# Keeping a bf16 copy of streamed weights in HBM for later tiles, and a shorter chain to the first matmul, in an eight-core decoder step

## The chip, the cores and the metric

The kernel runs on all 8 cores of one Trainium2 chip. The time of a run is that of the slowest core, in microseconds of the device. A program on all 8 cores has a slower state, in which one die (cores 0 to 3, or 4 to 7) is granted a lower TensorE clock; such runs are named slow, and only fast runs are compared here.

## The reference

The reference is one inference step of a two-layer decoder. Each core takes one prompt of 2048 tokens; the 32 decode sequences of 8 tokens are shared out as well, so that each core has a small group of 32 sample tokens. Cut to what matters:

```python
D_MODEL = 1024; SEQ = 2048; FFN_DIM = 2688; GLA_RANK = 16

def rmsnorm(x, g):
    y = x * rsqrt(mean(x * x, axis=-1) + EPS); return y * g
def swiglu_ffn(x, w_in, w_out):
    g, u = split(x @ w_in, 2); return (silu(g) * u) @ w_out
# layer 0
x += 0.5 * swiglu_ffn(rmsnorm(x), ...)            # fi0, fo0 in the kernel's names
x += gla_mixer(rmsnorm(x), ...)                    # v, qk, r, o; a gate of low rank 16
x += 0.5 * swiglu_ffn(rmsnorm(x), ...)            # fi1, fo1
k, v = shared_kv(x, ...)                           # kv
# layer 1
x += 0.5 * swiglu_ffn(rmsnorm(x), ...)            # fi2, fo2
x += dilated_window_attention(rmsnorm(x) @ wq, k, v) @ wo
x += 0.5 * swiglu_ffn(rmsnorm(x), ...)            # fi3, fo3
# in the GLA: log_a = log_sigmoid((h @ w_lowrank) @ w_g2 + b) / 16
```

All inputs and all outputs are fp32; the kernel multiplies in bf16.

## The kernel before

The prompt of a core is cut into four tiles of 512 tokens, t0 to t3, which run in pairs: t0 with t1, then t2 with t3. In each pair the even tile leads by up to 24 weight units. The sample tile of 32 tokens uses the units of t0. Every tile needs every weight, and SBUF does not hold them, so each tile streams all of them from HBM. A unit is 128 partitions by 2048 columns (2688 for the FFN's output weights). A load issued by GpSimd (POOL) casts it from fp32 to bf16 on the way, into one of two rings of 12288 columns, one for even tiles and one for odd ones. A slot of the ring comes free when its users (`users`: one tile, or t0 and the sample tile) are done.

The order of the instructions on each engine is fixed when the program is built, by a scheduler with a cost model. So an edit can change the order of everything after it.

The units and their loads (cuts are marked `# ...`):

```python
    for t in range(4):
        def add_unit(kind, i, src, n, users=0, t=t):
            u = Unit(src, n, users or (1 if t else 2), (t, kind, i))
            u.kind = kind
            units[(t, kind, i)] = u
            order[t % 2].append(u)
# ...
    first = {(0, "fi0", k): [("x", "b0", 2 * k + 1)] for k in range(4)}
    for k in range(4):
        first[(1, "fi0", k)] = [units[(0, "fi0", 12 + 2 * k)].key]

    def weights(slot):
        # ... take the next stretch of the ring, wait until the units in it are done with
            yield need(lambda over=over: all(o.left == 0 for _, _, o in over))
        # ...
            yield O(PL, (lambda e, u=u, dst=dst: e.dma_start(out=dst, in_=u.src)),
                    first.get(u.uid, []), writes=[u.key], cost=1.0, dma="w%d_%d" % (slot, k % NWS), nbytes=u.n * 512)
            u.ready = True
```

The start: x of a tile is loaded in four parts by SP, squared by ACT, summed by a chain of DVE adds, and the sum over partitions is one matmul with ones:

```python
    def load_x(T, prev):
        # ...
            yield O(SP, (lambda e, q=q, w=w, src=src, ms=ms: e.dma_start(
                out=T.x[:, ms[0]:ms[-1] + 1, :].rearrange("p m n -> p (m n)"), in_=src[:, q * w:(q + 1) * w])),
                [after.key] if T.t == 1 else [], writes=[xk(T, m) for m in ms], cost=0.1, dma="x%s_%d" % (T.b, q), nbytes=w * 512)
        for m in range(8):
            yield from square(T, m)      # ACT square; for 512 tokens a DVE add to the running sum

    def norm_stats(T):
        # ...
        ms = [T.sum] if n == 512 else range(8)
        yield mm(PS[b][:, 0:n], [(ones, T.h[:, m, :]) for m in ms], [hk(T, m) for m in ms] + ["ONE"], b, n)
```

The low-rank gate and the sample tile's GLA output:

```python
    def gla(T):
        # ... 8 matmuls of 16 output columns, then 4 with 16 rows of contraction
        yield from mmh(T, (PS[b][0:16, :],), lambda kt, z: WLR[:, kt, :], ["WLR"], (b,), n)
        # ...
                yield mm(PS[b], [(WG2[0:16, hd * 128:(hd + 1) * 128], glr)], [gk, "WG2"], b, n)
    # sample tile, for each s of 4 groups of 8 tokens:
                for hd in range(4):
                    for f in range(2):
                        e.matmul(po[:, hd * 2 + f, :], lhsT=vv[:, hd * 256 + f * 128:hd * 256 + (f + 1) * 128], rhs=am[:, hd, c8], start=True, stop=False)
                        ins = e.matmul(po[:, hd * 2 + f, :], lhsT=S0b[:, hd, f * 128:(f + 1) * 128], rhs=qT[:, hd, c8], start=False, stop=True)
```

The softmax here doesn't subtract the row's maximum and nothing guards it: scores larger than these inputs give would overflow.

## Time and profile before

| | before |
|---|---|
| time, median of 3 runs | 2364.44 us (2363.14 to 2366.65) |
| HBM read, written, per core | 662.88 MB, 15.40 MB |
| TensorE busy, core 0 | 2306.4 of 2359.6 us |

The profile was taken of a run in the slow state, so I read core 0, which is on the die that kept its clock. The view of the cores gives the span and the mean granted clock of each:

```profile
core 0: 2359.6 us, clock 0.993
...
die 1 (median of its cores): 2576.0 us, clock 0.897
```

The page of core 0 of the kernel before. Part 1 is busy time with its share of the span. The DMA row gives the busy share of the 16 DMA engines in 40 equal slices, in tenths. Part 3 gives the queues (q0 is the casting loads that POOL issues, q1 the plain transfers) with packets, MB and share, and the HBM traffic of the core. Part 6 gives loads with their size and median time from issue to landing.

```profile
PE 2306.4 (98%) x14660; PEld 1129.2 (48%) x14660; DVE 1219.9 (52%) x2180; ACT 1172.5 (50%) x2316; POOL 317.2 (13%) x599
...
DMA  9996898888988989988999988888899989598793
...
q0 software_dynamic: 84032, 326.10, 83.6%
q1 hardware_dynamic: 17120, 28.25, 4.0%
...
HBM read 662.88 MB, written 15.40 MB: 287 GB/s over the span
...
ring<-wfi POOLq DMA_DIRECT2D x336, 512.0 KB, 9.1
```

TensorE is busy 98% of the span, and the DMA engines are about as busy for most of it. Two limits lie close together.

The table of stretches of core 0. Its columns are the stretch, its length, the busy time (and number of instructions) of PE, of its weight loads, DVE, ACT and POOL, then the granted clock, the DMA share and GB/s moved, counted at the SBUF side:

```profile
0.00:118.00 118.00, 97.42 (x741) 48.04 (x742) 60.89 (x129) 68.32 (x167) 22.00 (x45) 1.00 1.00 177
20.00:120.00 100.00, 98.03 (x726) 48.09 (x726) 53.82 (x114) 61.80 (x147) 14.95 (x29) 1.00 1.04 179
1250.00:1420.00 170.00, 157.40 (x770) 75.02 (x767) 62.62 (x94) 56.99 (x94) 21.14 (x40) 0.96 0.89 159
```

From 20 to 120 us the DMA share is 1.04 (the view adds up the times of the packets, so a full stretch can come out a little above 1). There the pair has just begun, and the ring of each tile is being filled. In the same stretch, the view of the DMA queues says what was moved (MB at the SBUF side; a q0 byte in bf16 is two bytes at HBM):

```profile
q0 software_dynamic: 4377, 15.61, 95.7%
q1 hardware_dynamic: 576, 2.10, 7.6%
...
ring<-wfi POOLq DMA_DIRECT2D x25, 512.0 KB, 14.0
```

That is 15.61 MB of weights and 2.10 MB of x.

The view of the waits of TensorE on core 0: what it waited for, us in total, times, longest.

```profile
PE pst L615 <- DVE h L628: 12.7, 2, 10.5
PE pst L615 <- DMA ring<-wfo: 12.2, 3, 10.1
...
PE pst L615 <- DMA ring<-wfi: 5.7, 6, 2.4
```

Of the first line, 10.5 us are the start, from a first small matmul at 7.4 us to 18.2 us. The view puts this wait down to the chain of adds, which ended at 18.1 us, but the first weights landed at 18.1 us too. Of the second, 10.1 us are a single stall: the timeline of TensorE (start, us, instruction, and in brackets the idle time before it with what ended it) shows it at 1333 us.

```profile
1314.81 8.58 PE L615 MATMUL pst<-r,ring 128*128 128x512 bf16 x39
1333.48 16.04 PE L615 MATMUL pst<-r,ring 128*128 128x512 bf16 x63 [10.09 <-DMA ring<-wfo]
```

For accounts of where time goes I use one more number, worked out from the matmul starts in the trace. Matmuls of 512 columns that run back to back start 216 ns apart. The **excess** is the sum of what the gaps between starts have over that figure (in proportion for fewer columns, 2.2 ns and 2.4 columns a ns, and not under 25 ns). It counts waits and slow matmuls alike. All of the core's matmuls at these gaps make 2269.3 us.

### The profile page before, as it was taken

To read this page: it belongs to the slowest core of one execution; us is meant where nothing else is said; L and a number is where in the kernel's file an instruction comes from. 1 tells how busy PE (TensorE), PEld (TensorE's weight loads), DVE (VectorE), ACT (ScalarE), POOL (GpSimd) and SP (SyncE) were. 2 spreads that over 40 slices of the span, in tenths; PEclk is the share of its full clock that TensorE was granted. 3 is DMA by queue.
4 is the path that set the end of the run, shared out by engine and by line. 5 is a ranking of instruction groups with operands and counts; after the bars stand their busy time and mean duration, and the time that the engine had idled before them with its cause. 6 is when DMAs were issued, how large, how long until landed. Compare 5 with 4: busy or idle time off the path is not lost.

```text
span 2589.4 us, 42668 instructions; the slowest of 8 cores (2351.7 to 2589.4 us)
## 1 busy us (share of the span) xinstructions
PE 2542.9 (98%) x14660; PEld 1190.5 (46%) x14660; DVE 1223.3 (47%) x2180; ACT 1177.0 (45%) x2316; POOL 317.7 (12%) x599
## 2 busy tenths in 40 slices
PE   7999999999999999999999989999999999999999
PEld 3445444544444444455444435444544444444444
DVE  4424464445533446646543243454466335653742
ACT  5524544463443246455453124533555533753642
POOL 1111111101111111111111011011111111111110
PEclk8888888888888889999998878888999999999999
DMA  9986788778867788998897787667789989689794
GB/s 190 150 122 108 128 133 120 113 105 122 135 115 127 123 146 146 169 159 134 157 156 133 151 139 125 108 117 114 137 153 166 167 153 172 116 138 156 145 173 93
DMA packets 101362, 357.08 MB, mean 138 GB/s; under 512 B 12528, under 2 KB 17440, under 8 KB 101024
## 3 DMA queue, kind: packets, MB, share of 16 engines
q0 software_dynamic: 84032, 326.10, 77.7%
q1 hardware_dynamic: 17120, 28.25, 3.6%
q8 instruction: 122, 2.00, 0.3%
q14 instruction: 88, 0.72, 0.1%
HBM read 662.88 MB, written 15.40 MB: 262 GB/s over the span
## 4 chain that ended last, share of the span: by engine, by line
PE 96%; DMA 3%; issue 1%; ACT 0%; DVE 0%; SPq 0%; ACTq 0%; POOL 0%; POOLq 0%; DVEq 0%
PE pst L615 92%; DMA ring<-wfo 1%; DMA ring<-wfi 1%; PE pst L1410 1%; DMA ring<-ck 0%; PE pst L1349 0%; PE pst L987 0%; PE pst L970 0%; PE pst L988 0%; PE pst L1371 0%; DMA x<-xp 0%; PE pst L1433 0%; PE pst L1375 0%; PE pst L957 0%; PE pst L863 0%
## 5 line engine op out<-in xcount | busy, mean ns | idle before, releaser
L615 PE MATMUL pst<-h,ring 128*128 128x512 bf16 x6144 | 1531.1, 410 | 4.1 <-DVE h L631 3.3
L615 PEld LDWEIGHTS pst<-h,ring 128*128 128x128 bf16 x6144 | 623.5, 103 | 804.9 <-issue 471.8
L615 PE MATMUL pst<-r,ring 128*128 128x512 bf16 x3136 | 780.9, 409 | 6.4 <-DMA ring<-wfo 6.4
L620 ACT ACTIVATE pb<-pb 128x512 f32<-128x512 f32 x856 | 534.8, 629 | 64.7 <-DVE pb L823 4.4
L620 ACT ACTIVATE pb<-pst 128x512 f32<-128x512 f32 (+1 forms) x472 | 278.8, 595 | 567.6 <-PE pst L615 560.7
L628 DVE TENSOR_TENSOR pb<-pb,pst 128x512 f32<-128x512 f32 x368 | 252.2, 686 | 547.3 <-ACT pb L620 539.4
L615 PEld LDWEIGHTS pst<-r,ring 128*128 128x128 bf16 x3136 | 318.5, 103 | 415.6 <-issue 232.7
L511 POOL DMA_DIRECT2D ring<-wfi x336 | 178.0, 530 | 1224.4 <-PE pst L615 1150.7
L620 ACT ACTIVATE h<-x 128x512 bf16<-128x512 f32 x192 | 119.0, 627 | 391.3 <-DVE x L631 305.0
L628 DVE TENSOR_TENSOR r<-pb,pst 128x512 bf16<-128x512 f32 x336 | 230.6, 687 | 46.2 <-DVE pb L628 40.3
L631 DVE SCALAR_TENSOR_TENSOR x<-pst,x 128x512 f32<-128x512 f32 x128 | 88.3, 690 | 261.7 <-PE pst L615 261.4
L631 DVE SCALAR_TENSOR_TENSOR h<-x,CF,pb 128x512 bf16<-128x512 f32 x224 | 150.8, 746 | 13.4 <-ACT pb L620 12.6
L511 POOL DMA_DIRECT2D ring<-wfo x128 | 67.7, 529 | 605.5 <-PE pst L615 496.7
L628 DVE TENSOR_TENSOR pb<-pb,h 128x512 f32<-128x512 f32 x120 | 82.4, 689 | 43.7 <-ACT h L620 42.6
L615 PE MATMUL pst<-ring,h 128*128 128x256 bf16 x640 | 86.9, 302 | 0.0
L620 ACT ACTIVATE spb<-pst 128x32 f32<-128x32 f32 (+2 forms) x111 | 21.7, 198 | 125.0 <-PE pst L615 124.4
L615 PEld LDWEIGHTS pst<-ring,h 128*128 128x128 bf16 x640 | 67.4, 107 | 18.6 <-issue 5.1
L615 PEld LDWEIGHTS pst<-hsb,ring 128*128 128x128 bf16 x1536 | 53.9, 97 | 40.6 <-issue 35.4
L615 PE MATMUL pst<-hsb,ring 128*128 128x32 bf16 x1536 | 54.4, 178 | 14.1 <-DMA ring<-wfi 14.0
L511 POOL DMA_DIRECT2D ring<-wgl x64 | 33.9, 531 | 260.7 <-PE pst L615 238.9
L624 ACT COPY r<-pst 128x512 f32<-128x512 f32 (+3 forms) x104 | 51.0, 491 | 23.6 <-PE pst L1375 11.4
L628 DVE TENSOR_TENSOR x<-x,pst 128x512 f32<-128x512 f32 x64 | 43.9, 686 | 29.8 <-PE pst L615 29.7
(151 smaller groups left out, 1113.6 us busy)
## 6 DMA issues: line engine op xcount, KB each, us to landing
ring<-wfi POOLq DMA_DIRECT2D x336, 512.0 KB, 7.4
ring<-wfo POOLq DMA_DIRECT2D x128, 672.0 KB, 8.0
ring<-wgl POOLq DMA_DIRECT2D x64, 512.0 KB, 6.7
x<-xp SPq DMA_DIRECT2D x16, 512.0 KB, 9.6
y_p<-x SPq DMA_DIRECT2D x32, 256.0 KB, 7.8
ring<-wqd POOLq DMA_DIRECT2D x12, 512.0 KB, 9.7
ring<-wod POOLq DMA_DIRECT2D x16, 384.0 KB, 8.8
ring<-wkv POOLq DMA_DIRECT2D x8, 512.0 KB, 8.3
```

The lines of the kernel that those rows point to most:

```text
L511: yield O(PL, (lambda e, u=u, dst=dst: e.dma_start(out=dst, in_=u.src)), first.get(u.uid, []), writes=[u.key], cost=1.0, dma="w%d_%d" % (s ...
L615: ins = e.matmul(out, lhsT=l, rhs=r, start=(start and i == 0), stop=(stop and i == last), skip_group_check=skip)
L620: return O(ACT, lambda e: e.activation(out=out, in_=in_, func=func, scale=scale, bias=bias), reads, writes, c_act(n))
L624: return O(ACT, lambda e: e.copy(out=out, in_=in_), reads, writes, c_act(n))
L628: return O(DVE, lambda e: e.tensor_tensor(out=out, in0=a, in1=b, op=op), reads, writes, c_dve(n, rate))
L631: return O(DVE, lambda e: e.scalar_tensor_tensor(out=out, in0=a, scalar=s, in1=b, op0=op0, op1=op1), reads, writes, c_dve(n))
L1410: ins = e.matmul(PS[bs[hp]][0:nk, rr * 64 + jj * 32:rr * 64 + jj * 32 + 32], lhsT=KT[hp * 64:hp * 64 + 64, jj, sl_(r, nk, 16)], rhs=T.QT[h ...
```

## The change

The intent: the sum of the weight bytes that the four tiles read is large, and it is read as fp32. After the change tile 0 reads fp32 and, as each unit lands, writes it back to HBM in bf16 (`keep`, issued by SP). Tiles 1 to 3 load the bf16 copies. A unit of tile 0 now has a third user, its copy, so its ring slot is held until the copy is done.

Three smaller parts go with it. The first squares alternate between ACT and DVE and are summed by eight ones-matmuls in place of the chain of adds, and x of tile 0 is loaded by the SP and ACT queues by turns. The low-rank gate's eight matmuls go to four groups of 32 output columns, and the four that follow contract over 128 rows. The sample GLA's 64 alternating matmuls become 8 and 32 of one shape each.

The diff, cut to its core (cuts are marked `...`):

```diff
-            u = Unit(src, n, users or (1 if t else 2), (t, kind, i))
+            u = Unit(src, n, users or (1 if t else 3), (t, kind, i))
             u.kind = kind
+            u.copy = None
+            if not users:
+                if t == 0:
+                    u.copy = nc.dram_tensor("bf_%s_%d" % (kind, i), [128, n], BF16, kind="Internal").ap()
+                else:
+                    u.src = units[(0, kind, i)].copy
...
+    def keep(u, k):
+        yield O(SP, lambda e: e.dma_start(out=u.copy, in_=u.ap), [u.key], [("bf",) + u.uid[1:]], cost=0.1, dma="k%d" % (k % NWS), nbytes=u.n * BFB)
+        u.left -= 1
...
+            bf = u.uid[0] > 0
             yield O(PL, (lambda e, u=u, dst=dst: e.dma_start(out=dst, in_=u.src)),
-                    first.get(u.uid, []), writes=[u.key], cost=1.0, dma="w%d_%d" % (slot, k % NWS), nbytes=u.n * 512)
+                    first.get(u.uid, []) + [("bf",) + u.uid[1:]] * bf, writes=[u.key], cost=1.0, dma="w%d_%d" % (slot, k % NWS),
+                    nbytes=u.n * (BFB if bf else 512))
+            if u.copy is not None:
+                TH.spawn(keep(u, k), -31)
...
-            yield O(SP, (lambda e, q=q, w=w, src=src, ms=ms: e.dma_start(
+            yield O(ACT if T.t == 0 and q % 2 else SP, (lambda e, q=q, w=w, src=src, ms=ms: e.dma_start(
...
+        if T.t == 0:
+            T.sum = None
+            for m in range(8):
+                if m % 2:
+                    yield stt(T.h[:, m, :], T.x[:, m, :], 1.0 / 1024, T.x[:, m, :], ALU.mult, ALU.mult, T.n, [xk(T, m)], [hk(T, m)])
+                else:
+                    yield act(T.h[:, m, :], T.x[:, m, :], AF.Square, T.n, [xk(T, m)], [hk(T, m)], scale=1.0 / 32)
+                done.add(("sq", T.nm, 0, m))
+            return
...
-        ms = [T.sum] if n == 512 else range(8)
-        yield mm(PS[b][:, 0:n], [(ones, T.h[:, m, :]) for m in ms], [hk(T, m) for m in ms] + ["ONE"], b, n)
+        ms = [T.sum] if n == 512 and T.sum is not None else range(8)
+        for m in ms:
+            yield mm(PS[b][:, 0:n], [(ones, T.h[:, m, :])], [hk(T, m), "ONE"], b, n, start=(m == ms[0]), stop=(m == ms[-1]))
...
-        yield from mmh(T, (PS[b][0:16, :],), lambda kt, z: WLR[:, kt, :], ["WLR"], (b,), n)
+        hn = T.hn
+        for kt in range(8):
+            yield need(lambda: ("h", T.nm, hn, kt) in done)
+            p = slice(kt % 4 * 32, kt % 4 * 32 + 32)
+            yield O(PE, (lambda e: e.matmul(PS[b][p, :], lhsT=WLR[:, kt, :], rhs=T.h[:, kt, :], start=(kt < 4), stop=(kt >= 4))),
+                    [hk(T, kt), "WLR"], [("ps", b)], 0.06)
...
-                yield mm(PS[b], [(WG2[0:16, hd * 128:(hd + 1) * 128], glr)], [gk, "WG2"], b, n)
+                yield mm(PS[b], [(WG2[:, hd * 128:(hd + 1) * 128], glr)], [gk, "WG2"], b, n)
...
+                ins = e.matmul(PS[b][:, m * n:(m + 1) * n], lhsT=vv[:, m * 128:(m + 1) * 128], rhs=am[:, m // 2, :], start=True, stop=True)
...
-                        e.matmul(po[:, hd * 2 + f, :], lhsT=vv[:, hd * 256 + f * 128:hd * 256 + (f + 1) * 128], rhs=am[:, hd, c8], start=True, stop=False)
-                        ins = e.matmul(po[:, hd * 2 + f, :], lhsT=S0b[:, hd, f * 128:(f + 1) * 128], rhs=qT[:, hd, c8], start=False, stop=True)
+                        ins = e.matmul(po[:, hd * 2 + f, :], lhsT=S0b[:, hd, f * 128:(f + 1) * 128], rhs=qT[:, hd, c8], start=True, stop=True)
```

More of the change, by code (lines that the diff above doesn't have):

```diff
@@ L321, in build @@
     wfi = din("wfi", [4 * NF, 128, 2048]); wfo = din("wfo", [32, 128, 2688])
-    wgl = din("wgl", [16, 128, 2048]); wlr = din("wlr", [128, 128]); gg2 = din("gg2", [16, 512])
+    wgl = din("wgl", [16, 128, 2048]); wlr = din("wlr", [128, 256]); gg2 = din("gg2", [128, 512])
     wkv = din("wkv", [2, 128, 2048]); wqd = din("wqd", [3, 128, 2048]); wod = din("wod", [4, 128, 1536])
@@ L338, in build @@
     SM = A("SM", [128, 8], F32)
-    WLR = A("WLR", [128, 8, 16], BF16)
-    WG2 = A("WG2", [16, 512], BF16)
+    WLR = A("WLR", [128, 8, 32], BF16)
+    WG2 = A("WG2", [128, 512], BF16)
     U = A("U", [128, 4, 256], F32)
@@ L480, in build @@
     NWS = 8
+    BFB = 280
     first = {(0, "fi0", k): [("x", "b0", 2 * k + 1)] for k in range(4)}
@@ L805, in gla @@
         (b,) = yield from get_banks(1)
-        yield from mmh(T, (PS[b][0:16, :],), lambda kt, z: WLR[:, kt, :], ["WLR"], (b,), n)
+        hn = T.hn
[4 more added lines that the diff above has]
+                    [hk(T, kt), "WLR"], [("ps", b)], 0.06)
         (gi,) = yield from pool.get("glr", 1, 1)
-        glr, gk = pool.aps[gi][0:16, 0:256].bitcast(BF16), pool.key(gi)
-        yield copy(ACT, glr, PS[b][0:16, :], n, [("ps", b)], [gk])
+        glr, gk = pool.aps[gi][:, 0:256].bitcast(BF16), pool.key(gi)
+        yield copy(ACT, glr, PS[b], n, [("ps", b)], [gk])
         put(b)
@@ L1029, in gla_s @@
         (b,) = yield from get_banks(1)
-        yield from mmh(T, (PS[b][0:16, 0:n],), lambda kt, z: WLR[:, kt, :], ["WLR"], (b,), n)
+        yield from mmh(T, (PS[b][0:16, 0:n],), lambda kt, z: WLR[:, kt, 0:16], ["WLR"], (b,), n)
         glr = KB[0:16, 896:928]
@@ L1093, in gla_s, with fi @@
         gv = [rk(T, ("gv", hd)) for hd in range(4)]
+        (b,) = yield from get_banks(1)
+        def fi(e):
+            ins = None
+            for m in range(8):
+                ins = e.matmul(PS[b][:, m * n:(m + 1) * n], lhsT=vv[:, m * 128:(m + 1) * 128], rhs=am[:, m // 2, :], start=True, stop=True)
+            return ins
+        yield O(PE, fi, [gk] + gv, [("ps", b)], c_mm(8, n))
+        yield copy(ACT, oT.rearrange("p m n -> p (m n)"), PS[b][:, 0:8 * n], 8 * n, [("ps", b)], [rk(T, "go")])
+        put(b)
         for s in range(4):
@@ L1106, in fo @@
                     for f in range(2):
-                        e.matmul(po[:, hd * 2 + f, :], lhsT=vv[:, hd * 256 + f * 128:hd * 256 + (f + 1) * 128], rhs=am[:, hd, c8], start=True, stop=False)
-                        ins = e.matmul(po[:, hd * 2 + f, :], lhsT=S0b[:, hd, f * 128:(f + 1) * 128], rhs=qT[:, hd, c8], start=False, stop=True)
-                return ins
-            yield O(PE, fo, [gk, ub.key] + gv, [("ps", b)], 1.68)
-            yield copy(ACT, oT[:, :, c8], po, 64, [("ps", b)], [rk(T, "go")])
+                        ins = e.matmul(po[:, hd * 2 + f, :], lhsT=S0b[:, hd, f * 128:(f + 1) * 128], rhs=qT[:, hd, c8], start=True, stop=True)
+                return ins
+            yield O(PE, fo, [gk, ub.key], [("ps", b)], 0.3)
+            yield tt(oT[:, :, c8], oT[:, :, c8], po, ALU.add, 64, [("ps", b), rk(T, "go")], [rk(T, "go")])
             put(b)
@@ L1585, in prologue @@
         yield O(PL, lambda e: e.dma_start(out=CB[:, 128:], in_=cbd[:, :]), [], ["CB"], cost=1.0, dma="c1", nbytes=(B_END - 128) * 512)
-        yield O(PL, lambda e: e.dma_start(out=WG2[:], in_=gg2[:, :]), [], ["WG2"], cost=1.0, dma="c2", nbytes=32768)
-        yield O(PL, lambda e: e.dma_start(out=WLR[:].rearrange("p a b -> p (a b)"), in_=wlr[:, :]), [], ["WLR"], cost=1.0, dma="c3", nbytes=65536)
+        yield O(PL, lambda e: e.dma_start(out=WG2[:], in_=gg2[:, :]), [], ["WG2"], cost=1.0, dma="c2", nbytes=262144)
+        yield O(PL, lambda e: e.dma_start(out=WLR[:].rearrange("p a b -> p (a b)"), in_=wlr[:, :]), [], ["WLR"], cost=1.0, dma="c3", nbytes=131072)
         yield O(SP, lambda e: e.dma_start(out=stabs[:], in_=rsd[:, :]), [], ["stabs"], cost=0.1, dma="c4", nbytes=32768)
@@ L1638, in make_in_maps @@
     shared = {
-        "wfi": f(wfi), "wfo": f(wfo), "wgl": f(wgl), "wlr": f(cols(glr, 8).reshape(128, 128)), "gg2": f(inp["gla_w_gate2"])[0],
+        "wfi": f(wfi), "wfo": f(wfo), "wgl": f(wgl), "wlr": f(np.pad(cols(glr, 8), ((0, 0), (0, 0), (0, 16))).reshape(128, 256)),
+        "gg2": f(np.tile(np.pad(f(inp["gla_w_gate2"])[0], ((0, 16), (0, 0))), (4, 1))),
         "wkv": f(np.stack([cols(kvw[:, i * 256:(i + 1) * 256], 8).reshape(128, 2048) for i in range(2)])),
```

## The prediction

> **What bounds the kernel now.** I read core 0, on the fast die of a slow run (2359.6 us, clock 0.993, view of the cores). TensorE is busy in 2306 of those us (table of stretches). 512-column matmuls start 216 ns apart; costing every matmul by its columns, I estimate 2286 us of bare TensorE work. About 60 us remain, beside 7 before the first matmul and 6 after the last:
> - start: tile 0's first FFN matmul runs at 22 us;
> - a 10.1 us wait for a wfo load (waits of TensorE) up to 1333 us, at a DMA share of 1.03; with the slow restart 16 us;
> - the sample GLA's 64 eight-column matmuls, 108 ns each, 7 us;
> - smaller DMA waits at 500 to 1000 us, 10 us.
>
> DMA is the second limit: in 22 to 115 us its share is 1.04, at 175 to 188 GB/s written, twice that read. The Trainium skill, "HBM Reference", Specifications, gives a core 358 GB/s; the trace agrees, at 360. A 512 KB unit (1 MB of fp32) then takes 2.9 us; TensorE uses one in 3.9 us, with the sample's matmuls.
>
> **What the change does.**
> 1. Tiles 1 to 3 read 2 bytes an element instead of 4; tile 0 writes 2 more. While tiles 0 and 1 run together HBM bytes are unchanged (4+2+2 against 4+4); in packets, 4 KB cast ones take 324 ns (median), plain ones 172: 668 against 648. In the second half the load halves.
>  - Removed: the stall at 1323 us, both tiles there now bf16: -15 us. Small DMA waits: -5.
>  - Added: at first tile 0 runs nearly alone. A unit costs 1.5 MB of HBM traffic, estimated 4.4 us against TensorE's 3.9. For 15 to 20 units TensorE becomes DMA-bound, until tile 1's cheap loads mix in: +6 us (0 to +15).
> 2. Start. TensorE sums the squares, in place of a DVE chain that ended at 18.1 us. But the first weights still wait for x, and the first two units land at 18.2 and 21.6 us, as the normalised x is ready (21.7). So only part counts: -3.
> 3. Low-rank gate: 8 matmuls of 16 output columns, 219 ns apart, become two sets of four in separate column groups. "TensorE: Matmul & The Clock Gate", Part 3, says that such tiles run concurrently; no run here shows it. From 7.9 us in all to some 2.5: -5. The 16-row gate matmuls (317 ns apart, 16) become 128-row ones (216): -1.5.
> 4. Sample GLA: 64 alternating 32- and 128-row matmuls become 8 and 32 of one shape: -5.
>
> **Sum.** -15 -5 +6 -3 -6.5 -5 = -28.5. Predicted **2336 us** (-1.2%), range **2312 to 2360**. Chances: faster by over 2% 0.13, within 2% 0.83, slower 0.04.
>
> **What would show it.** HBM reads fall from 663 to about 427 MB, writes rise from 15 to 94. DMA share in the second half about 0.5, no DMA wait of TensorE over 1 us there, none near 1320 us. Waits for wfi in 20 to 110 us grow from 0.3 us to several. First FFN matmul at 18 to 20 us. Gate matmuls on WLR about 60 ns apart.
>
> **What would make it wrong.** The added term is the least certain: copies may hold ring slots longer or slow the loads through the whole first half (+20), or the static order mixes tile 1 in early enough for no cost (-6). Column groups may not overlap (+5).

## The result, and the profile after

Ratios here and below are the mean time of one kernel's fast runs over that of the other's in the same rounds, so they are not quite the ratios of the medians that are quoted.

| | before | after |
|---|---|---|
| time, median | 2363.79 us (4 runs) | 2383.05 us (4 runs, one of them slow; the ratio also uses a fifth, fast run of 2379.07 us) |
| ratio of the fast runs | 1 | 1.0071, 95% interval 1.0052 to 1.0090 |
| HBM read, written | 662.88, 15.40 MB | 427.24, 94.04 MB |
| first matmul of 512 columns on FFN weights | 22.1 us (core 0; 20.0 to 22.1 over the cores) | 21.7 us (core 0; 19.8 to 22.2 over the cores) |

The change is slower, by 0.7%, where 1.2% faster had been predicted. The interval lies clear of 1, and the time lies outside the predicted range.

The profile after is of a fast run, and I read core 7, the slowest:

```profile
core 7: 2376.0 us, clock 0.985
die 0 (median of its cores): 2364.5 us, clock 0.989
```

The page of core 7 after the change, with the lines that answer to those above:

```profile
PE 2312.0 (97%) x14643; PEld 1130.3 (48%) x14643; DVE 1216.5 (51%) x2181; ACT 1166.6 (49%) x2309; POOL 317.1 (13%) x599
...
DMA  9999699988898989997755544444554563354452
...
HBM read 427.24 MB, written 94.04 MB: 219 GB/s over the span
...
ring<-wfi POOLq DMA_DIRECT2D x84, 512.0 KB, 14.0
...
ring<-bf_fo_3 POOLq DMA_DIRECT2D x12, 672.0 KB, 4.8
```

The traffic is just what was predicted: reads 427 MB, writes 94 MB. The DMA row falls to 4 to 6 tenths in the second half. Note the line of `ring<-wfi`: the fp32 loads, now only tile 0's, take 14.0 us to land where they took 9.1.

The stretches of core 7:

```profile
0.00:118.00 118.00, 81.05 (x574) 37.37 (x575) 46.73 (x102) 50.51 (x130) 16.19 (x34) 0.90 0.95 215
20.00:120.00 100.00, 78.03 (x567) 36.49 (x568) 43.73 (x93) 45.63 (x115) 9.51 (x18) 0.88 1.01 227
1250.00:1420.00 170.00, 170.00 (x834) 80.52 (x832) 69.36 (x103) 63.57 (x106) 22.69 (x44) 1.00 0.53 174
```

The stretch near 1320 us is now full (170.00 of 170.00 us, before 157.40), at a DMA share of 0.53. But in the first 118 us TensorE is busy 81.05 us where it was 97.42, and the granted clock there is 0.90 where it was 1.00. The DMA share is about 1 in both.

The DMA queues of core 7 from 20 to 120 us:

```profile
q0 software_dynamic: 3290, 11.03, 67.1%
q1 hardware_dynamic: 3307, 11.55, 33.3%
...
ring<-wfi POOLq DMA_DIRECT2D x15, 512.0 KB, 15.0
x<-xp SPq DMA_DIRECT2D x4, 512.0 KB, 21.1
```

Two of the loads on q0 are bf16 units (1.05 MB). So HBM carried 2 × 9.98 + 1.05 for the loads, and 11.55 for x (2.10) and copies (9.4): 32.6 MB, against 33.3 before. **The memory carried as much as before, but 9.4 MB of it were copies, and the weights that landed fell from 15.6 to 11.0 MB.** The Trainium skill, "HBM Reference", Specifications, gives a core about 358 GB/s; this trace is near it, at 326 to 333 GB/s, reads and writes added.

The waits of TensorE on core 7:

```profile
PE pst L632 <- DMA ring<-wfi: 16.8, 8, 6.4
...
PE pst L632 <- DVE h L645: 8.7, 1, 8.7
PE pst L632 <- DMA ring<-wfo: 3.9, 3, 3.3
```

The waits for `wfi` grew from 5.7 to 16.8 us (from 20 to 120 us alone, from 2.7 to 12.9), and the 10.1 us wait for `wfo` is gone. The wait of 8.7 us for h ends at 96 us, so it is new in the early stretch as well: it is the sum of squares of tile 1, whose x took 21.1 us to land (last line of the view of the queues above). A piece of the timeline of TensorE shows what such a wait can cost; its last two lines are from later on the same core:

```profile
36.33 0.55 PE L632 MATMUL pst<-hsb,ring 128*128 128x32 bf16 x16 [2.56 <-DMA ring<-wfi]
36.73 5.30 PE L632 MATMUL pst<-h,ring 128*128 128x512 bf16 x16
...
55.70 0.59 PE L632 MATMUL pst<-hsb,ring 128*128 128x32 bf16 x16 [6.36 <-DMA ring<-wfi]
56.12 6.00 PE L632 MATMUL pst<-h,ring 128*128 128x512 bf16 x16
...
62.37 3.61 PE L632 MATMUL pst<-h,ring 128*128 128x512 bf16 x16
...
618.42 0.55 PE L632 MATMUL pst<-hsb,ring 128*128 128x32 bf16 x16 [2.56 <-DMA ring<-wfi]
618.82 3.61 PE L632 MATMUL pst<-h,ring 128*128 128x512 bf16 x16
```

Sixteen matmuls of 512 columns take 3.61 us (the line at 62.37). After the wait of 2.56 us the same sixteen take 5.30 us, and after that of 6.36 us 6.00 us: of the first ten, most start 427 ns apart and not 216. The Trainium skill, "TensorE: Matmul & The Clock Gate", Part 1, describes this: after idling, the array runs at half rate for some microseconds. The trace agrees, but not after every wait: after another one of 2.56 us, at 618 us, the sixteen take 3.61 us. On core 7, from 20 to 120 us, six gaps of over 0.8 us between 512-column matmuls make 22.8 us of excess, and 43 matmuls at half rate another 8.8 us; before it was 11 such matmuls, 2.2 us, and no such gap.

The account of the whole, in us: the time to the first matmul, then the excess. Core 0 is taken for both, so that the same core is compared; in brackets the range over the six cores after the change whose trace has all matmuls.

| stretch, us | before, core 0 | after, core 0 (range) | difference |
|---|---|---|---|
| to the first matmul | 7.4 | 12.8 (11.0 to 12.8) | +5.4 |
| to 120 | 16.5 | 40.9 (32.5 to 40.9) | +24.4 |
| 120 to 290 | 12.0 | 1.2 (1.2 to 3.7) | -10.8 |
| 290 to 420 | 1.4 | 6.3 (5.5 to 10.8) | +4.9 |
| 420 to 1250 | 17.8 | 24.8 (15.9 to 24.8) | +7.0 |
| 1250 to 1420 | 18.3 | 0.8 (0.3 to 2.9) | -17.5 |
| 1420 to the end, with the tail after the last matmul | 17.2 | 18.1 (17.8 to 19.3) | +0.9 |
| matmuls at full rate | 2269.3 | 2270.2 | +0.9 |
| sum | 2359.9 | 2375.1 | +15.2 |

The sums agree with the spans, 2359.6 and 2374.7 us. So the gains came (near 1320 us, and from 120 to 290 us, where the sample GLA makes 5.6 of the 10.8 us), and the start, +29.8 us with its two rows, gave them all back. The question for the experiments is why the start costs 25 us or more where the prediction had 6.

### The profile page after: what moved, and what is told of

It reads as the page before. It is cut to its first block, busy times and chain, and to the rows that moved or that the text cites. A ratio compares the mean times of both kernels' runs of the same rounds, so it can differ in the third digit from the quotient of the medians.

```text
span 2376.0 us, 43134 instructions; the slowest of 8 cores (2353.5 to 2376.0 us)
## 1 busy us (share of the span) xinstructions
PE 2312.0 (97%) x14643; PEld 1130.3 (48%) x14643; DVE 1216.5 (51%) x2181; ACT 1166.6 (49%) x2309; POOL 317.1 (13%) x599
## 3 DMA queue, kind: packets, MB, share of 16 engines
q10 hardware_dynamic: 288, 1.05, 0.2%
HBM read 427.24 MB, written 94.04 MB: 219 GB/s over the span
## 4 chain that ended last, share of the span: by engine, by line
PE 91%; DMA 6%; DVE 1%; issue 1%; ACT 1%; POOL 0%; SPq 0%; DVEq 0%; ACTq 0%; POOLq 0%
PE pst L632 87%; DMA ring<-wfi 3%; DMA x<-xp 2%; DMA ring<-wfo 1%; PE pst L1453 1%; PE pst L1392 0%; DMA sts<-ring 0%; DMA ring<-wgl 0%; PE pst L1414 0%; PE pst L1004 0%; PE pst L1021 0%; DVE h L648 0%; PE pst L1022 0%; PE pst L1476 0%; ACT pb L637 0%
## 5 line engine op out<-in xcount | busy, mean ns | idle before, releaser
L632 PE MATMUL pst<-h,ring 128*128 128x512 bf16 x6144 | 1392.6, 382 | 3.2 <-DMA ring<-wgl 1.6
L632 PEld LDWEIGHTS pst<-h,ring 128*128 128x128 bf16 x6144 | 592.6, 98 | 710.0 <-issue 43.2
L632 PE MATMUL pst<-r,ring 128*128 128x512 bf16 x3136 | 711.5, 381 | 0.0
L632 PEld LDWEIGHTS pst<-r,ring 128*128 128x128 bf16 x3136 | 303.2, 98 | 358.7 <-issue 11.0
L525 POOL DMA_DIRECT2D ring<-wfi x84 | 44.5, 533 | 255.3 <-PE pst L632 155.9
L632 PE MATMUL pst<-ring,h 128*128 128x256 bf16 x640 | 75.4, 275 | 0.0
L632 PE MATMUL pst<-hsb,ring 128*128 128x32 bf16 x1536 | 53.3, 177 | 18.9 <-DMA ring<-wfi 16.8
L637 ACT ACTIVATE h<-pst 128x512 bf16<-128x512 f32 (+4 forms) x96 | 47.2, 514 | 19.3 <-PE pst L1392 11.0
L637 ACT ACTIVATE spb<-spb 128x32 f32<-128x32 f32 (+2 forms) x194 | 44.5, 230 | 14.7 <-ACT spb L637 0.8
```

The source lines that it names most:

```text
L632: ins = e.matmul(out, lhsT=l, rhs=r, start=(start and i == 0), stop=(stop and i == last), skip_group_check=skip)
L637: return O(ACT, lambda e: e.activation(out=out, in_=in_, func=func, scale=scale, bias=bias), reads, writes, c_act(n))
```

## The experiments

Three theories compete for the early loss:

- **Bytes.** Early on the memory has no spare time, so each byte of a copy pushes out a byte of a weight load.
- **Slots.** The copies hold ring slots longer, so loads are issued later; the number of bytes matters little.
- **Order.** The changed costs in the scheduler's model give another order of the program, and that order is worse.

Each kernel differs from the changed one only by the edits shown. All results were correct, all fast-run ratios are against the kernel before on the same chip, and all runs had five rounds. Line numbers in profile lines shift by some lines from kernel to kernel.

### No copies: e1_no_copy

Tile 0 writes nothing, all tiles load fp32; the start, the gate and the sample GLA stay changed.

```diff
-                if t == 0:
+                if False:
                     u.copy = nc.dram_tensor(...)
-                else:
+                elif False:
                     u.src = units[(0, kind, i)].copy
-            u = Unit(src, n, users or (1 if t else 3), (t, kind, i))
+            u = Unit(src, n, users or (1 if t else 2), (t, kind, i))
-            bf = u.uid[0] > 0
+            bf = False
```

> The change without its copies: all four tiles load fp32, and the shorter start, the gate matmuls and the sample GLA stay. Copy theories (bytes, or ring slots held): the idle time of TensorE in the first 118 us falls from 37 us back to about 20, the 10 us wait for a wfo load near 1320 us comes back, and the time is 2345 to 2358 us, below before. Start theory (x on two queues delays the first weights) or reorder theory (the new static order itself is worse): the time stays at 2370 us or above and the idle time in the first 118 us above 30 us.

Measured: ratio 0.9968 (0.9955 to 0.9981); its median, 2417 us, holds four slow runs of eight. TensorE is busy 94 to 101 us of the first 118, the excess to 120 us is 14 to 20 us, and the stall near 1320 us is back (13 to 15 us). So the early loss belongs to the copies and the cure of the late stall belongs to them as well. The rest of the change gains 0.3%.

### The first 18 units not copied: e3_skip18

```diff
+            skip = kind == "fi0" and i < 18
-            u = Unit(src, n, users or (1 if t else 3), (t, kind, i))
+            u = Unit(src, n, users or (1 if t else 2 if skip else 3), (t, kind, i))
-            if not users:
+            if not users and not skip:
```

(and `bf` is true only for a unit whose source is a copy)

> The change, but the first 18 FFN units, which tile 0 loads while it runs nearly alone, are not copied; tiles 1 to 3 read those 18 in fp32. Copy theories (bytes or slots): TensorE busy in the first 118 us rises from 81 to 95 us or more, no stall near 1320 us, and the time is 2330 to 2348 us (ratio to before 0.985 to 0.993). Start or reorder theory: within 6 us of the change as it is (about 2377 to 2383).

Measured: 2358.37 us, ratio 0.9977 (0.9965 to 0.9989). TensorE is busy 96 to 101 us of the first 118, as without copies. Near 1320 us the excess is 2 to 7 us. At 290 to 420 us it is 8 to 10 us, though, and the time is a miss: 2330 to 2348 us had been expected. The early loss is thus due to the copies of the very first units; but the other copies together gain nothing against no copies at all (0.9977 against 0.9968).

### x on one queue: e4_one_queue

```diff
-            yield O(ACT if T.t == 0 and q % 2 else SP, (lambda ...
+            yield O(SP, (lambda ...
```

> The change, but tile 0's x is loaded from the SP queue alone, as before. Start theory: the first weight unit is issued at about 10.5 instead of 12.2 us, lands near 18 us, and the time falls by 8 us or more. Bytes theory: the first FFN matmul comes 1 to 3 us earlier, but the stalls that follow take it back; the time changes by less than 4 us and TensorE busy in the first 118 us stays below 86 us.

Measured: 2375.49 us, ratio 1.0044 (1.0031 to 1.0057), against 1.0071 with two queues (on another chip), some 6 us less, between the marks that I had set for the two theories. It is not clear of noise: the two intervals overlap, and the other pairs that differ in the queues, also on different chips, give less or the reverse (without copies 0.9968 with two queues, e1, and 0.9958 and 0.9977 with one, e14 and e19; with 18 units uncopied 0.9977, e3, and 0.9987, e6). What the traces show is the start. The first matmul starts at 5.6 to 7.2 us where it started at 11.0 to 12.8, and the first one on FFN weights at 17.3 to 18.7 us where it was at 19.8 to 21.7. So the two queues delay the start by some 3 us; what they cost in all is not settled. The Trainium skill, "DMA: Bandwidth & Descriptors", section "Issuing engines are not separate DMA queues", says that transfers issued by several engines interleave on the same DMA engines and that only issue time is saved. The trace agrees: on two queues the two parts of x that ACT issued land first, at 8.80 and 11.57 us, and those of SP at 12.67 and 13.89 us (core 0 after the change), where before all four land in their order, at 9.89, 11.20, 12.47 and 13.63 us (core 0). So the last part comes no sooner, and the first one later, as it is one of SP's. The sample's x lands at 10.93 instead of 4.68 us, and the first weight load, which waits for the first part of x, is issued at 13.28 instead of 10.49 us.

### A write of the same bytes that holds no slot: e5, e9, e10

Here the first 18 units are not copied (as in e3), and each of them, when it has landed, sets off a write to HBM from tile 0's h buffer: as many bytes as the copy had (e5), half (e9), or an eighth (e10). No ring slot waits for it.

```diff
+    def fake(u, k):            # e5: 4 of h's 8 slices; e9: 2; e10: 256 columns of one
+        yield O(SP, lambda e: e.dma_start(out=scratch, in_=hb[0][:, 0:4, :]),
+                [landed(u)] + [h of tile 0], [], dma="k%d" % (k % NWS), nbytes=u.n * BFB)
```

> As the run that skips 18 copies, but each of those 18 units, once landed, sets off a write of as many bytes to HBM out of another tensor, so that it uses the DMA engines and HBM like a copy and holds no ring slot. Bytes theory: the early stall is back, TensorE busy in the first 118 us at 78 to 87 us and the time at least 12 us above the run without the writes. Slot theory (copies hold ring slots too long, bytes are harmless): busy at 93 us or more and the time within 5 us of the run without the writes.

> The same with every write cut to one half. Bytes theory with a threshold (a unit costs HBM time only where it exceeds TensorE's 3.9 us; half a copy makes it some 3.7 to 4.1): the time is closer to the run with small writes than to the one with full writes, at most 16 us above the former. Bytes theory without a threshold: half way between. Order theory: within 8 us of the full writes.

> The run with loose writes, with every one of the 18 writes cut to an eighth (512 bytes a partition for 4096); the order of every instruction on every engine is the same as in that run, only the size of these DMA differs. Bytes theory: the early stall is gone, TensorE busy in the first 118 us is 94 us or more, and the time is 2350 to 2366 us, at least 28 us under the run with full writes. Order theory (the static order of that run is itself worse): within 8 us of the run with full writes.

Measured: ratios 1.0134, 1.0082 and 1.0064 (intervals 1.0119 to 1.0149, 1.0069 to 1.0095 and 1.0048 to 1.0081). These runs failed as a test. DVE writes tile 0's next h into that same buffer, so it has to wait for the write to be done, and the trace shows it: TensorE waits 11.8 us for DVE's h in e10, and the chain of waits passes from the write to DVE. That wait is an artefact of the source that I chose, and it stays even with an eighth of the bytes. The falling ratio fits bytes, but does not show it.

### The same writes from a buffer that nobody overwrites soon: e11_writes_x and e12_tiny_x

The source is now x of tile 0, which is not rewritten in that stretch. e11 writes the bytes of a copy (4096 per partition), e12 an eighth (512). Both have the same instructions in the same order on every engine, and no slot is held in either. So they differ in bytes alone.

```diff
-        src = hb[0][:, 0:4, :]
+        src = xb[0][:, 0:2, :] flattened, columns 0:1024 (e11) or 0:128 (e12), fp32
```

> The same, in the same order of instructions on every engine, with full writes of 4096 bytes a partition, no ring slot held. Bytes theory: at least 10 us above the run with small writes, and most of the change's early stall (TensorE busy in the first 118 us at 80 to 88 us). Slot theory: within 5 us of the run with small writes, busy at 94 us or more.

> Mends a fault of the three runs with loose writes: their writes read tile 0's h, and the profile shows DVE waiting for them before it could overwrite h, a wait of my own making. Here the writes read tile 0's x, which nothing overwrites in that stretch; 18 units not copied, small writes of 512 bytes a partition. Bytes theory and slot theory: as the run that skips 18 copies, 2352 to 2364 us, TensorE busy in the first 118 us at 95 us or more. Order theory: 2370 us or more.

Measured, on a chip whose time before was 2376.34 us: e11 2398.99 us, ratio 1.0087 (1.0067 to 1.0107); e12 2373.37 us, ratio 0.9982 (0.9962 to 1.0002). The stretches and the DMA queues of core 0, of e11 first:

```profile
0.00:118.00 118.00, 81.61 (x550) 37.20 (x560) 47.84 (x102) 52.47 (x128) 16.76 (x35) 0.93 0.97 208
```

```profile
q0 software_dynamic: 3279, 11.00, 69.7%
q1 hardware_dynamic: 3051, 10.63, 31.3%
...
ring<-wfi POOLq DMA_DIRECT2D x18, 512.0 KB, 19.7
```

and of e12:

```profile
0.00:118.00 118.00, 93.35 (x687) 44.74 (x700) 54.41 (x118) 61.35 (x152) 20.47 (x42) 0.97 0.96 175
```

```profile
q0 software_dynamic: 3949, 13.44, 83.5%
q1 hardware_dynamic: 3696, 4.75, 17.1%
...
ring<-wfi POOLq DMA_DIRECT2D x23, 512.0 KB, 17.4
```

With the full bytes TensorE is busy 81.61 us of the first 118, as with the real copies (81.05 after the change), with an eighth 93.35 (79 to 86 and 93 to 98 over all cores), and the excess to 120 us is 33 to 41 us on its cores, the range after the change; with an eighth it is 17 to 21 us. HBM carried 2 × 11.00 + 10.63 = 32.6 MB in e11 and 2 × 13.44 + 4.75 = 31.6 MB in e12: again the sum hardly moves and the weights make room. **This shows the cause of the early loss: the bytes written.** Held slots are not needed for it, and order is excluded, as it is the same in both. The copies of e11 cost 25 us (1.0087 less 0.9982, of 2376 us).

The trace also names a path by which late bytes delay weights. Tile 1's four x loads are marked as readers of tile 0's units 3, 5, 7 and 9 (`[after.key]` in `load_x`, before and after alike), so those slots come free only when x has landed. From 20 to 120 us POOL waited for such x loads 5.6 us before and 35.0 us after, 42.3 us in e11 and 10.4 us in e12. As the DMA share is near 1 in all four, I count this as a form of the shortage of bytes; no run takes the marking away. In the changed kernel POOL also waited 16.5 us there for copies to give their slots back, which e11 does not have; as e11 loses as much, these waits need not have cost anything.

### Tile 1 mixed in earlier: e8_early_tile1

If tile 0 alone is what makes copies dear, tile 1 with its cheap loads should come sooner.

```diff
-        first[(1, "fi0", k)] = [units[(0, "fi0", 12 + 2 * k)].key]
+        first[(1, "fi0", k)] = [units[(0, "fi0", 4 + 2 * k)].key]
```

> The change, with tile 1's first loads released by tile 0's units 4, 6, 8, 10 in place of 12, 14, 16, 18, so that the cheap bf16 loads and their matmuls can mix in sooner. Bytes theory: fewer idle us early (TensorE busy in the first 118 us at 84 us or more) and 4 to 15 us less in all. Slot or order theory: no change beyond 4 us either way.

Measured: 2382.87 us, ratio 1.0014 (0.9992 to 1.0037). That is 0.6% under the changed kernel's ratio, on another chip. But the busy time of the first 118 us is only 75 to 87 us, so the gain is not where it was expected. This run settles nothing but that the loss is not cured this way.

### Which copies pay: e6, e7, e13, e16, e17

All have x on one queue, and differ in what is copied:

```diff
e6:   skip = kind == "fi0" and i < 18
e7:   skip = kind not in ("fi3", "fo3")                          # the last FFN alone
e13:  skip = kind not in ("fo0", "v", "qk", "r", "o")            # 24 units
e16:  skip = kind == "fi0" and i < 18 or kind == "fi1"
e17:  skip = not (kind == "fi0" and i >= 18 or kind in ("fo0", "v", "qk", "r", "o"))   # 27 units
```

> The first 18 copies skipped and tile 0's x loaded from the SP queue alone. If the two costs are apart, the time is that of the run that skips 18 copies less the 5 to 6 us that one queue gained: 2350 to 2355 us, the first FFN matmul at 17 to 19 us. If the first is hidden by the second: no gain, about 2358 us.

Measured: 2356.17 us, ratio 0.9987 (0.9949 to 1.0025). The interval is wide, as one fast run took 2380.93 us.

> Only the 29 units of the last FFN are copied (the ones that tile 1 loads in the stretch of the old stall near 1320 us), and x comes on one queue. If copies cost where tile 0's loads already fill the DMA, and the gain is that stall alone: the stall at 1320 us is at most 3 us, the first half is as in the run without copies, and the time is 2332 to 2346 us (ratio 0.986 to 0.992). If the halved loads of the whole second half matter: 2350 us or more.

Measured: 2373.9 us, ratio 1.0037 (1.0024 to 1.0051), a miss. The stall near 1320 us stays whole, and 860 to 1130 us, where these copies fall, has 23 to 26 us of excess where the others have 3 to 16. But the waits of TensorE from 860 to 1130 us on core 0 are for DVE and ACT, 14 us in all, and none for a DMA, so this loss is not shown to be one of bytes. The wait near 1320 us is for a `wfo` load, though the loads of tile 1's last FFN are now bf16. So I now took it to be not the end of tile 1, which I had held in the expectation of this run, but tile 2's first output projection `fo0`, whose loads then meet the first loads of tile 3; e13 and e18 below test that:

```profile
PE pst L635 <- DMA ring<-wfo: 9.9, 1, 9.9
```

> The run that copied only the last FFN kept the stall near 1320 us: the load it waits for is tile 2's own first output projection, in fp32 there, next to tile 3's first loads. Here only tile 0's first output projection and its GLA weights are copied (24 units, after the early stretch), x on one queue. If that stall comes from tile 2's loads: it falls from 16 us to 8 or less, the rest is as in the run without copies, and the time is 2336 to 2350 us. If it stays, the time is 2350 to 2358 us.

Measured: 2361.74 us on the slower chip (before 2376.34), ratio 0.9928 (0.9902 to 0.9953), the best of all. The start is whole (99 to 103 us busy of the first 118), and the excess near 1320 us falls to 5 to 8 us, which fits `fo0` (the GLA weights were copied with it). In the profiled run the granted clock of die 1 is lower than that of die 0 (0.988 and 0.993, median of its cores), so this time is not quite that of an undisturbed run.

> The first 18 units and all 21 units of the second FFN's input projection are not copied, the other copies stay, x on one queue. If the copies of the second FFN are what slows 290 to 420 us (idle 4 us per core there against 0 to 2 without copies): excess of TensorE there falls from 8 to 9 us to 5 or less, and the time is 3 to 8 us under the run that skips 18 only (ratio 0.9987, so about 0.996). If it is the order: within 2 us of it, the excess there at 8 us.

Measured: 2357.31 us, ratio 0.9959 (0.9944 to 0.9974). The ratio fell as if the copies of `fi1` were to blame, but the excess of 290 to 420 us stays at 9 to 10 us with the `fi1` units uncopied. So that excess is not their copying; it appears in some orders of the program and not in others.

> Only the 27 units from unit 18 of the first FFN to the end of the GLA are copied, x on one queue: a try for the best version. As the run with 24 copies or a little better: 0.990 to 0.995 of before, stall near 1320 us at 8 us or less, TensorE busy in the first 118 us at 98 us or more.

Measured: 2364.02 us with two slow runs, ratio 0.9967 (0.9946 to 0.9989), a miss (0.990 to 0.995 expected) and no better than e13.

### No copies, one queue: e14_no_copy_one_queue

> No copies at all, all four tiles load fp32, tile 0's x on one queue; the compute parts stay. If the copies of tile 0's first output projection and GLA are what gains over the rest: 0.994 to 0.997 of before (about 2350 to 2358 us), with the stall near 1320 us at 13 to 18 us, and above the two runs with 24 and 27 copies by 5 to 12 us. If the copies gain nothing net: as low as those, 0.993 or less.

Measured: 2357.94 us, ratio 0.9958 (0.9944 to 0.9973), with the stall near 1320 us back at 13 to 15 us, and only 0.2 to 1.2 us at 290 to 420 us. So, without any copy, the rest of the change is worth about 0.4%, 10 us.

### The copies alone on the kernel before: e2_copy_only

The diff is the copying part of the change, put on the kernel before; start, gate and sample GLA are as before.

> The kernel before with the copies alone: tile 0's units are written back in bf16 and tiles 1 to 3 load those; start, gate and sample GLA stay as they were. If the parts add up, this is the changed kernel's 1.0071 less what the other parts give together. The other parts with one queue gave 0.9958, with two queues 0.9968 (an earlier run without copies), so the copies alone should cost 1.0086 to 1.0113 of the time before. TensorE busy in the first 118 us near 83 to 87 us (before 96 to 100), excess over column cost up to 120 us 33 to 40 us, and at 1250 to 1420 us under 2 us. The theory in the prediction (copies cost 6 us and save 20) would give 0.994 and a busy time of 93 or more.

Measured: ratio 1.0111 (1.0075 to 1.0147), with three slow runs of six; the fast ones took 2381 to 2401 us. The excess to 120 us is 37 to 40 us and near 1320 us 0.3 to 1.7 us; four of the six cores read lose another 13.6 us at 120 to 200 us, which the whole change does not. There TensorE waits for nothing; its granted clock is 0.81 on these four cores (2 to 5, on both dies), and 512-column matmuls start 260 ns apart. With the neighbouring stretches 566 matmuls of core 2 ran so, which cost it some 26 us. It is the fast run of 2401.06 us that was profiled; the other two took 2382.60 and 2381.27 us, and these two alone give a ratio of 1.0084. The waits of TensorE on core 0, which kept its clock, its stretch, and then a stretch of core 2:

```profile
PE pst L630 <- DMA ring<-wfi: 23.6, 9, 9.7
```

```profile
0.00:118.00 118.00, 83.68 (x598) 39.48 (x609) 51.98 (x111) 57.25 (x141) 17.82 (x37) 0.93 0.99 221
...
120.00:140.00 20.00, 20.00 (x121) 9.01 (x120) 7.71 (x16) 10.98 (x24) 1.80 (x4) 0.81 1.02 254
```

The parts add up: 1.0111 (copies alone) times 0.9968 (the rest alone) is 1.0079, and the whole gave 1.0071; with 1.0084 for the copies it is 1.0052, the lower end of the whole's interval.

### Does copying 24 units pay at all: e18 and e19

e13 and e14 had run on different chips, so both were run again in one call: e18 is the kernel of e13, e19 that of e14.

> The best kernel so far, only tile 0's first output projection and the GLA weights copied, x on one queue; earlier 0.9928 on another, slower chip. If copying these 24 units pays for itself, it stays under the kernel without copies of this same call by 0.2% or more: 0.991 to 0.995. If the copies' net is nothing, both come out alike within 0.2%, near 0.996, and the earlier difference was the chip.

> No copies, x on one queue, the compute parts: 0.9958 earlier. Expected 0.9945 to 0.9975 again, whatever the chip, as it reads and writes as the kernel before does.

Measured: e18 2352.3 us, ratio 0.9958 (0.9943 to 0.9973); e19 2355.64 us, ratio 0.9977 (0.9962 to 0.9992), just above what was expected. Set directly against each other, their means are 2352.4 and 2356.4 us, a ratio of 0.9983 with a 95% interval of about 0.9970 to 0.9996, worked out from the spread of the runs. The copies of these 24 units gain some 4 us, a little less than I had set as the mark. What they buy is a part of the stall near 1320 us. The view of the waits of TensorE of each kernel between 1250 and 1420 us, core 0, e18 and then e19:

```profile
PE pst L635 <- DMA ring<-bf_fo: 3.9, 1, 3.9
```

```profile
PE pst L632 <- DMA ring<-wfo: 9.4, 1, 9.4
```

The wait falls from 9.4 to 3.9 us here (7.7 to 4.1 on core 1) and does not vanish. In e18 the first loads of tile 3 that compete with it are still fp32, which may be why: with those copied too (the whole change) the excess near 1320 us is 0.3 to 2.9 us, and with 18 of them uncopied (e3) 2 to 7. Both kernels beat the one before, and e18's is the fastest found: 0.4% by this call, 0.7% by the earlier one on a slower chip, and below the changed kernel by about 1.1% (0.9958 against 1.0071, different chips).

A summary of the ratios, by what is copied:

| copied | start, gate, sample GLA | x queues | ratio to before |
|---|---|---|---|
| all (e2) | as before | one | 1.0111 (1.0084 without the run of low clock) |
| all (the change) | changed | two | 1.0071 |
| all (e4) | changed | one | 1.0044 |
| last FFN (e7) | changed | one | 1.0037 |
| all but the first 18 (e3, e6) | changed | two, one | 0.9977, 0.9987 |
| none (e1) | changed | two | 0.9968 |
| none (e14, e19) | changed | one | 0.9958, 0.9977 |
| 24 units (e13, e18) | changed | one | 0.9928, 0.9958 |

## Why the prediction was wrong

**The step that failed** is the added term in step 1 and in the sum: "A unit costs 1.5 MB of HBM traffic, estimated 4.4 us against TensorE's 3.9. For 15 to 20 units TensorE becomes DMA-bound [...] +6 us (0 to +15)". Measured, TensorE lost 24 us more than before from its first matmul to 120 us (the 5.4 us before that are the two queues, as they are gone in e4), and the pair of runs that differ in written bytes alone (e11, e12) shows 25 us for them. The term was mis-sized by a factor of four, and by itself this moves the sum of -28.5 to about -10.

The mistake is in what the copies were set against. I compared a unit's load, 2.9 us, with TensorE's 3.9 us per unit, and so took 1 us per unit as free time of the memory. Yet the same text reads a DMA share of 1.04 from 22 to 115 us: the memory had no free time there. The surplus was already in use, for filling both rings, for tile 1's x (2.10 MB) and for tile 1's first weights. Weights of 15.61 MB are 29.8 units in 100 us, more than the 25.6 that TensorE takes at 3.9 us. The right estimate was at hand: copies of 9.4 MB at the 333 GB/s read from that stretch take 28 us, and where the share is already 1 all of it is delay. The rate was a little lower, too: 333 GB/s, not the 360 that I had by doubling all of the moved bytes, x's fp32 bytes among them. On top come the restarts at half rate, 8.8 us of the excess of core 7 in that stretch against 2.2 before; these were not in the sum at all, though they lie within the measured loss.

Point by point:

- **Traffic** (427 MB read, 94 MB written, half share in the second half): right, and it is the part that decided least. "HBM bytes are unchanged" while two tiles run together was right as well, but it takes an average over the whole pair. At the head of the pair tile 0 runs alone, reads at full price, and writes.
- **The stall near 1320 us** (-15): right in size, 18.3 to 0.8 us. My reason, the two tiles there, was right in that both then load bf16; which units stall (tile 2's `fo0` with tile 3's first loads) came out only through e7. The gain near 1320 us was real, but the start had cost more than that before.
- **Small DMA waits at 500 to 1000 us** (-5): not gained. From 420 to 1250 us the excess is 17.8 before and 15.9 to 24.8 after. In the first half the DMA share is as high as before (the DMA row shows 8 and 9 tenths), because there the copies are still being written.
- **Start** (-3): the first matmul of 512 columns on FFN weights came no earlier: at 20.0 to 22.1 us over the cores before and 19.8 to 22.2 after. The two queues for x hid the gain (e4): with one queue it comes at 17.3 to 18.7 us, some 3 us earlier, and then the term is about right. I had not costed the second queue at all.
- **Gate** (-6.5): the matmuls on 128 rows came as predicted, 5.1 to 3.5 us in all, 317 to 216 ns each. The low-rank ones gained only 0.7 us of the 5 on core 7 (7.9 on core 0 before, 7.2; 6.4 on core 0 after), worked out from their starts. The prediction took from the Trainium skill, "TensorE: Matmul & The Clock Gate", Part 3, that tiles in separate column groups run concurrently. The trace agrees: they start 3 to 5 ns apart where they follow each other. But the program sprinkles them among 128-wide matmuls, and a change from or to one mostly costs a gap of 308 to 323 ns where 216 is usual. For tile 1 they come as fast as DVE makes h, one in 662 ns:

```profile
397.30 0.57 PE L839 MATMUL pst<-h,WLR 128*32 128x512 bf16 x3
398.16 0.38 PE L839 MATMUL pst<-h,WLR 128*32 128x512 bf16 x1 [0.29 <-DVE h L648]
398.82 0.38 PE L839 MATMUL pst<-h,WLR 128*32 128x512 bf16 x1 [0.29 <-DVE h L648]
```

- **Sample GLA** (-5): right, 6.7 to 1.1 us; the eight-column matmuls that were 108 ns apart are 25 ns apart.
- **290 to 420 us**: not in the prediction, +5 to +9 us. It is absent without copies (e1, e14, e7) and there with others (e3, e16), also where the units of that stretch are not copied (e16). Of it, 1 to 2 us are the gate of tile 1, paced by DVE. On the cores of die 1 another 2.4 us are a lower granted clock (54 or 55 matmuls 260 ns apart; 0.91 on core 7 from 330 to 360 us), which die 0 does not have. The rest goes with the order of the program; which step of the order it is stays open.

Put together, the copies as a whole were to bring -14 us (-15 -5 +6). They cost 20 to 24 us: 1.0044 against 0.9958 (20 us, e4 and e14, different chips), 1.0071 against 0.9968 (24 us, the change and e1, different chips), and by themselves 1.0084 (20 us, the two runs of e2 without the low clock; 26 us, 1.0111, with the third). The other parts were to bring -14.5 us and brought 5 to 10 (e1, e14, e19).

The two ways in which the prediction named that it could be wrong included this one: "copies may [...] slow the loads through the whole first half (+20)". It was priced as a tail, and the DMA share that it quoted made it the most likely case.

What stays open: where the gain of e8 comes from; what the second queue for x costs in all; why e7 waits for DVE and ACT where its copies fall; the excess at 290 to 420 us beyond the gate; how much of the early loss goes by way of the slots that tile 1's x loads hold; and whether the limit there is the HBM itself or the 16 DMA engines, whose share was about 1 in all of these runs.

## What to carry to other kernels

Before adding traffic, read the DMA share of the stretch where it will fall, not of the whole span and not per unit of work: where it is already 1, count every added byte as a delay of its size over the measured rate (here 28 us by that sum, 25 measured). Bytes that are saved in another stretch help only where a wait ends there (here 17.5 us near 1320 us). A cache that is written while its first user runs alone costs most just when the pipeline fills; cache those units whose later loads stall something, and begin when there is slack (24 of the units, copied after the early stretch, gained some 4 us where all of them lost 20). For two experiments to tell bytes from order, keep the program the same and change the size of one transfer, from a buffer that nobody waits to overwrite.

## What the Trainium skill lacked or had wrong

- "HBM Reference", Specifications, gives one bandwidth per core and does not say how writes count beside reads. Here they added up in one budget: 333 GB/s of reads alone before, and 326 GB/s of reads and writes together after, in the same stretch (20 to 120 us). The share of the DMA engines was about 1 as well (1.04 and 1.01), so these runs do not tell which of the two sets that budget.
- "TensorE: Matmul & The Clock Gate", Part 3, describes tiles in separate column groups as concurrent, which the runs confirm (starts 3 to 5 ns apart), but gives no cost for changing between such tiles and full-width matmuls. "TensorEngine Tiling (Array Packing)", Key Properties, has that a change of tiling mode drains the array, without a figure. Here it was 308 to 323 ns between starts where 216 ns is usual, so scattered small tiles gained 0.7 us of an expected 5 (1.5 on core 0).
- "TensorE: Matmul & The Clock Gate", Part 1, gives an idle window of about 3.4 us before the array falls back to half rate, calls that window free-running, and gives no length for the shorter idle times that it also blames in one kernel. On core 7 a wait of 2.56 us that ended at 36 us was enough: the sixteen matmuls after it took 5.30 us and not 3.61, most of the first ten 427 ns apart. So was one of 2.04 us, at 71 us (5.21 us), but another of 2.56 us, at 618 us, was not (3.61 us).
- "DMA: Bandwidth & Descriptors", "Issuing engines are not separate DMA queues", says that several issuing engines only save issue time. It lacks that this can do harm: with x on two queues the other queue's parts landed first, at 8.80 and 11.57 us, and the first part at 12.67 us and not 9.89, so that the weight load that waited for it went out at 13.28 us and not 10.49 (core 0).
